# Reordering the seven products of a two-by-two block multiplication, and starting their weight sums with the stage

## The chip, the core and the metric

One core of a Trainium2 chip runs the whole program. The metric is the device time of one execution in microseconds (us). The kernel before takes 3117.28 us, the median of three runs (3116.49 to 3119.43).

The engines that matter here are TensorE (PE in the rows: matmuls, transposes), VectorE (DVE), ScalarE (ACT), GpSimd (POOL) and SyncE (SP). Each takes its own instructions strictly in the order in which they stand in its program; an instruction that waits holds up everything behind it on that engine. SP does nothing here but start the plain transfers, POOL starts the transfers that add to what is already in the buffer.

## What is computed

A network of six layers on 256 tokens of width 1024, in fp32: four layers of FFN, attention, FFN (eight FFNs) and two further layers of a mixer and one FFN each. All ten FFNs have the same core:

```
def swiglu(x, w_in, w_out):
    gate, up = jnp.split(x @ w_in, 2, axis=-1)
    return (jax.nn.silu(gate) * up) @ w_out
```

`w_in` is 1024 x 5632 (gate and up beside each other, 2816 columns each), `w_out` 2816 x 1024. Around it stand norms, residuals and, once in between, the attention or the mixer. 34.6 MB of weights are read for each FFN and used for 256 tokens only, so that the weights are streamed through the core once.

## The kernel before

**Precision.** A matmul runs on fp32r operands, which keep fewer bits than fp32. Each operand is therefore split into a high and a low part: ACT casts the high part (L171), DVE subtracts to get the low part (L172), and `mm3` issues three matmuls, high x high (L220), low weight x high x (L222) and high weight x low x (L224).

**Tiles.** The tokens form two tiles of 128 (t = 0, 1). The 2816 columns of an FFN are cut into 11 chunks of 256 (gate and up of a chunk make 512 columns, one PSUM bank). `f1(c, t)` multiplies tile t with chunk c, 24 matmuls, and starts a small task `hidden` (tanh on ACT at L414, two DVE steps at L416 and L417 that write `hd`, a transpose of `hd` on PE at L252, the split into `hT`). `f2` multiplies `hT` with 256 rows of `w_out` and adds into the accumulators aA (t = 0) and aB (t = 1), 12 matmuls.

**Seven products for eight.** Two pairs of neighbouring chunks of each FFN (4 and 5, 8 and 9) are not computed by `f1`. `seven(c)` takes tokens in two halves, the depth 1024 in two halves, and makes gate and up of both chunks and both tiles from seven products in place of eight. It needs seven sums of halves of x, made once per stage by `halves_of_x` (the tiles Sh and Sl, in the order 0, 1, 2, 3, 5, 4, 6), and for some products sums of quarters of the weights (a quarter is 512 deep x 512 wide, 1 MB). A sum of quarters is not computed by an engine: `load` (L449, SP) brings one quarter into a buffer `rs`, and `plus` (L454, POOL) starts two transfers of 512 KB that add another quarter to it in place. `split` casts the result, `block` multiplies it with one of the seven sums, 12 matmuls. The two `rs` buffers y and z go through chains: y is first B01+B00 (product 3), then another quarter is added (product 4), then another (product 2); z is B11 (product 6), then plus B01 (product 5). A `plus` has to wait until the split before it has read the buffer, and the next split has to wait until the `plus` has landed. Products 0 and 1 use single quarters, loaded into the common `raw` buffers.

**What sets the order.** In `ffn` a string gives the order around each seven: "fo7of7o7fo7of7o7o7o", where f is an `f1`, o an `f2` and 7 the next product. The products come in the order 0, 1, 3, 4, 6, 5, 2, and the first part of `seven` (load of y, first `plus`, load of z) runs just ahead of the string; for the first seven of a stage that is after the four opening `f1` (chunks 0 and 1, both tiles) and after `halves_of_x`. The tile framework then places each engine's instructions by its own cost model, so that the order on an engine is not the order of the text.

**Buffers.** Four `raw` buffers (RAW_BUFS) of 1 MB take all plain weights, seven hi/lo pairs (W_BUFS) the casts. `halves_of_x` uses an `rs` buffer for its scratch f (L582). In the stages behind the first, `ada_step` reads 1 MB of `w_ada` into a `raw` buffer twice per seven and multiplies it on DVE (L1182, L1184).

The sixteen stages (ten FFNs, four attentions, two mixers) are numbered from 0. The one shown below is stage 3, the second layer's first FFN, directly behind the first layer's last: its `f1` begin at 563 us of the profile and it ends near 750 us.

Of the kernel before, what the change touches and what calls it, by code (L numbers as in the profile page):

```python
# [18 lines left out]
P = 128  # L19
D = 1024  # L20
S = 256
# [13 lines left out]
UW = 1024  # L35

RAW_BUFS = 4
# [65 lines left out]
class _Net:  # L103
# [296 lines left out]
    def ffn(self, w_in, w_out, factors, finish, middle, scaled):  # L400
# [33 lines left out]
        def seven(c):  # L434
# [1 line left out]

            S = sums["S"]

            def quarter(k, n):
                return self.cols(w_in, c * FC + n * DFF, 512, 4 * k, 4)

# [8 lines left out]
            def plus(r, k, n):  # L452
                for q in range(2):
                    nc.gpsimd.dma_start(r[:, 2 * q : 2 * q + 2], quarter(k, n)[:, 2 * q : 2 * q + 2], accum_op=ALU.add)  # L454
# [8 lines left out]
                return ws  # L463

            def block(i, ws):
                ps = self.ps("mm")
                x = ([S[0][:, i, k] for k in range(4)], [S[1][:, i, k] for k in range(4)])
                for k in range(4):
                    self.mm3([(ps, slice(0, 512))], x, k, ws[k], k == 0, k == 3)
                return ps  # L470

            def add(dst, u, v):
                nc.vector.tensor_tensor(dst, u, v, op=ALU.add)

            def tile(ps=None):
                r = self.t(self.mp, [P, 512], "sc", bufs=3)
                if ps is not None:
                    nc.scalar.copy(r, ps)
                return r
# [13 lines left out]
            plus(y, 0, 0)  # L493
            z = load(1, 1)
            yield
            s = tile(block(0, split(load(0, 0, True))))
            yield
            g0 = self.t(self.fp, [P, 512], "res", bufs=2)
            add(g0, block(1, split(load(1, 0, True))), s)
            gate(g0)  # L500
            ws = split(y)
            plus(y, 1, 1)
            yield
            u1 = tile(block(3, ws))
            ws = split(y)
            plus(y, 1, 0)
            yield
            add(s, block(4, ws), s)
            u0 = tile()
            add(u0, s, u1)  # L510
            ws = split(z)
            plus(z, 0, 1)
            yield
            add(u0, block(6, ws), u0)
            self.start(out(0, g0, u0))
            yield
            add(s, block(5, split(z)), s)
# [11 lines left out]
            f2(c, t=t)  # L529

        first = ((0, 0), (0, 1), (1, 0), (1, 1)) if self.stage == 0 else ((0, 0), (1, 0), (0, 1), (1, 1))
        for c, t in first:
            f1(c, t)
        queue.extend((c, t) for c in range(2) for t in range(NT))
        self.start(self.halves_of_x(sums, scaled))
        for plain, c in PLAN:


            gen = seven(c)
            next(gen)  # L540
            others = [(r, t) for r in plain for t in range(NT)]
            for n, what in enumerate("fo7of7o7fo7of7o7o7o"):
                if what == "f":
                    f1(*others[0])
                    queue.append(others.pop(0))
                elif what == "o":
                    pop()
                else:
                    self.force(lambda: "S" in sums)
                    next(gen, 0)  # L550
                if n in (6, 15) and self.stage > 0:
                    self.ada_step()
            queue.extend((c + i, t) for i in range(2) for t in range(NT))
            if middle:
                middle()
                middle = None
# [8 lines left out]
    def halves_of_x(self, res, scaled):  # L565


        nc = self.nc
        if not scaled:
            fs = [self.prepared(t) for t in range(NT)]  # L570
            rb = self.t(self.mp, [P, NT, P], "rb")
            ps = self.ps("tp")
            for t in range(NT):
                nc.tensor.matmul(ps[:, t * P : t * P + P], fs[t][:, 0:1].to_broadcast([P, P]), self.ident,
                                 start=True, stop=True)
            nc.scalar.copy(rb, ps[:, :S].rearrange("p (a b) -> p a b", a=2))
        S_ = [self.t(self.mp, [P, 7, 4, P], f"S{n}", F32R) for n in "hl"]

        def put(i, v):
            self.hilo(v, S_[0][:, i], S_[1][:, i])  # L580

        f = self.t(self.mp, [P, 4, 512], "rs", bufs=2)  # L582
        x = {}
        for t in (0, 1):
            for k in (0, 1):
                xh, xl = (v[:, 4 * k : 4 * k + 4].bitcast(F32) for v in self.xT[t])
                v = x[t, k] = f[:, 2 * t + k].rearrange("p (a b) -> p a b", a=4)
                nc.vector.tensor_tensor(v, xh, xl, op=ALU.add)
                if not scaled:
                    nc.vector.tensor_tensor(v, v, rb[:, t, None, :].to_broadcast([P, 4, P]), op=ALU.mult)  # L590
        tt, stt = nc.vector.tensor_tensor, nc.vector.scalar_tensor_tensor
        put(0, x[0, 0])
        put(1, x[0, 1])
        put(2, x[1, 1])
        tt(x[1, 1], x[1, 1], x[1, 0], op=ALU.subtract)
        put(3, x[1, 1])
        tt(x[1, 0], x[0, 0], x[1, 0], op=ALU.subtract)
        put(5, x[1, 0])
        stt(x[0, 0], x[1, 1], -1.0, x[0, 0], op0=ALU.mult, op1=ALU.subtract)
        put(4, x[0, 0])  # L600
        stt(x[0, 1], x[0, 0], -1.0, x[0, 1], op0=ALU.mult, op1=ALU.subtract)
        put(6, x[0, 1])
        res["S"] = S_
        return
        yield
# [1005 lines left out]
```

## Time and profile before

| | us |
|---|---|
| median of three runs | 3117.28 (3116.49 to 3119.43) |
| the profiled execution, whole | 3114.58 |
| its span, first to last instruction | 3112.8 |
| PE busy | 2890.8 (93%) |
| DVE busy | 2177.3 (70%) |
| ACT busy | 1669.8 (54%) |
| POOL busy | 432.7 (14%) |
| mean granted TensorE clock | 0.967 |
| moved by DMA, mean over the span | 203 GB/s |

"Busy" is time in which an engine has an instruction under way. PE is idle for 222 us of the span. The granted clock is the share of full speed at which the chip lets TensorE run: it is 1.0 most of the time and 0.5 for some microseconds after some of the waits, so a mean of 0.967 is time lost too, beside the idle time and not in it.

### The profile page before, as it was taken

The page shows a single profiled execution, that of the slowest core. Times are in us where ns is not written, and L with a number is a line of the kernel's source. Part 1 is how long each engine was busy: PE and PEld are TensorE (multiplying, and loading weights), DVE is VectorE, ACT ScalarE, POOL GpSimd, SP SyncE. Part 2 cuts the span into 40 slices and gives each one's busy share as a digit, 9 for nine tenths or more (in the row PEclk, how much of TensorE's full clock was granted, in tenths as well). Part 3 has the DMA queues.
Part 4 walks back from the last instruction along what each step waited for, and adds up shares of the span by engine and source line. Part 5 has one row for each costly group of instructions (what it writes and reads, how often), then busy time and mean ns, then how long its engine had stood idle before and what let it go on. Part 6 is the DMA issues. An engine that isn't in the chain of part 4 may idle for free.

```text
span 3112.8 us, 36892 instructions
## 1 busy us (share of the span) xinstructions
PE 2890.8 (93%) x13165; PEld 2308.1 (74%) x13165; DVE 2177.3 (70%) x3275; ACT 1669.8 (54%) x2853; POOL 432.7 (14%) x601
## 2 busy tenths in 40 slices
PE   7999989999998998999989889998999998999888
PEld 6787767777786786778767768776778777788677
DVE  7675867767567686666867867586776687865766
ACT  5456645545665454456645545664555454644544
POOL 1112110111111011121100111211111011100110
PEclk9999999999999999999999999999999999999999
DMA  9754587786458778651687786458765589665784
GB/s 281 216 177 148 173 253 203 237 243 181 152 167 239 210 231 250 190 187 54 192 236 201 231 237 195 136 185 249 225 212 177 170 252 267 212 221 169 209 244 129
DMA packets 358043, 633.27 MB, mean 203 GB/s; under 512 B 15170, under 2 KB 190132, under 8 KB 357860
## 3 DMA queue, kind: packets, MB, share of 16 engines
q1 hardware_dynamic: 312724, 541.99, 50.9%
q0 software_dynamic: 44768, 88.30, 16.0%
q8 instruction: 104, 1.70, 0.2%
q14 instruction: 79, 0.65, 0.1%
q10 hardware_dynamic: 368, 0.62, 0.1%
HBM read 629.82 MB, written 1.05 MB: 203 GB/s over the span
## 4 chain that ended last, share of the span: by engine, by line
PE 52%; DMA 18%; issue 17%; DVE 7%; ACT 4%; POOL 2%; ACTq 0%; SPq 0%; POOLq 0%; DVEq 0%
DMA rs<-in_ffn_w_in_dram 13%; PE mm L222 10%; PE mm L224 10%; PE mm L220 10%; DVE lo L172 4%; DMA rs<-in_w_ffn_in_dram 4%; PE tp L252 3%; PE aA L222 2%; PE aA L220 2%; PE aA L224 2%; ACT hi L171 2%; PE aB L224 2%; PE aB L220 2%; PE aB L222 2%; DMA raw<-in_w_ada_dram 1%
## 5 line engine op out<-in xcount | busy, mean ns | idle before, releaser
L172 DVE TENSOR_TENSOR lo<-raw,hi 128x1024 fp32r<-128x1024 f32 x834 | 1004.2, 1219 | 240.4 <-ACT hi L171 232.5
L171 ACT CAST hi<-raw 128x1024 fp32r<-128x1024 f32 x834 | 867.2, 1050 | 393.9 <-PE mm L224 201.7
L220 PE MATMUL mm<-hi,xh 128*128 128x512 f32 (+2 forms) x1856 | 762.0, 412 | 112.6 <-ACT hi L171 112.0
L222 PE MATMUL mm<-lo,xh 128*128 128x512 f32 (+2 forms) x1856 | 747.5, 403 | 12.4 <-DVE lo L172 12.0
L224 PE MATMUL mm<-hi,xl 128*128 128x512 f32 (+2 forms) x1856 | 740.6, 399 | 2.0 <-DVE xl L172 1.0
L220 PEld LDWEIGHTS mm<-hi,xh 128*128 128x128 f32 x1856 | 359.1, 194 | 199.5 <-ACT hi L171 127.9
L222 PEld LDWEIGHTS mm<-lo,xh 128*128 128x128 f32 x1856 | 358.4, 193 | 102.8 <-DVE lo L172 36.8
L224 PEld LDWEIGHTS mm<-hi,xl 128*128 128x128 f32 x1856 | 358.3, 193 | 79.5 <-DVE xl L355 5.0
L171 ACT CAST hi<-rs 128x1024 fp32r<-128x1024 f32 x200 | 207.0, 1049 | 324.4 <-DMA rs<-in_ffn_w_in_dram 246.3
L172 DVE TENSOR_TENSOR lo<-rs,hi 128x1024 fp32r<-128x1024 f32 x200 | 241.6, 1221 | 187.9 <-ACT hi L171 186.1
L454 POOL DMA_DIRECT2D rs<-in_ffn_w_in_dram x128 | 155.9, 1285 | 1049.1 <-DVE lo L172 845.4
L220 PE MATMUL mm<-hi,Sh 128*128 128x512 f32 x560 | 229.0, 409 | 0.0
L222 PE MATMUL mm<-lo,Sh 128*128 128x512 f32 x560 | 223.1, 398 | 0.0
L224 PE MATMUL mm<-hi,Sl 128*128 128x512 f32 x560 | 222.2, 397 | 0.0
L220 PE MATMUL aB<-hi,hT 128*128 128x512 f32 x568 | 202.3, 417 | 0.0
L220 PE MATMUL aA<-hi,hT 128*128 128x512 f32 x584 | 198.2, 402 | 1.3 <-DVE s L658 0.9
L222 PE MATMUL aB<-lo,hT 128*128 128x512 f32 x568 | 198.9, 407 | 0.0
L224 PE MATMUL aB<-hi,hT 128*128 128x512 f32 x568 | 195.5, 405 | 0.9 <-DVE hT L268 0.8
L222 PE MATMUL aA<-lo,hT 128*128 128x512 f32 x584 | 193.0, 394 | 0.6 <-DVE lo L172 0.5
L264 ACT CAST hT<-tp 128x256 fp32r<-128x256 f32 x268 | 95.1, 371 | 183.3 <-PE tp L252 183.2
L224 PE MATMUL aA<-hi,hT 128*128 128x512 f32 x584 | 192.0, 392 | 0.0
L265 DVE TENSOR_TENSOR hT<-tp,hT 128x256 fp32r<-128x256 f32 x268 | 107.9, 417 | 53.2 <-ACT hT L264 52.7
(280 smaller groups left out, 3666.8 us busy)
## 6 DMA issues: line engine op xcount, KB each, us to landing
raw<-in_ffn_w_in_dram SPq DMA_DIRECT2D x224, 512.0 KB, 5.3
raw<-in_ffn_w_out_dram SPq DMA_DIRECT2D x88, 1024.0 KB, 7.1
rs<-in_ffn_w_in_dram POOLq DMA_DIRECT2D x128, 512.0 KB, 7.9
raw<-in_w_ada_dram SPq DMA_DIRECT2D x48, 1024.0 KB, 9.2
raw<-in_w_in_dram SPq DMA_DIRECT2D x44, 1024.0 KB, 5.2
rs<-in_ffn_w_in_dram SPq DMA_DIRECT2D x32, 1024.0 KB, 6.7
raw<-in_ffn_w_in_dram SPq DMA_DIRECT2D x32, 1024.0 KB, 6.8
raw<-in_w_ffn_in_dram SPq DMA_DIRECT2D x56, 512.0 KB, 4.9
```

The source lines that it names most:

```text
L171: self.nc.scalar.copy(hi, raw)
L172: self.nc.vector.tensor_tensor(lo, raw, hi.bitcast(F32), op=ALU.subtract)
L220: mm(ps, xh[k], wh[:, c], start=first, stop=False)
L222: mm(ps, xh[k], wl[:, c], start=False, stop=False)
L224: mm(ps, xl[k], wh[:, c], start=False, stop=last)
L252: self.nc.tensor.transpose(dst, src, self.ident[:k, :k])
L264: nc.scalar.copy(hi, v)
L265: nc.vector.tensor_tensor(lo, v, hi.bitcast(F32), op=ALU.subtract)
L454: nc.gpsimd.dma_start(r[:, 2 * q : 2 * q + 2], quarter(k, n)[:, 2 * q : 2 * q + 2], accum_op=ALU.add)
```

## The change

The seven products come in the order 6, 3, 0, 1, 4, 5, 2. Product 6 uses z as it was loaded and product 3 the first sum in y, and behind each of these two splits the next `plus` is started at once. Between product 3 and product 4 (the next link of y) now stand products 0 and 1, between 6 and 5 (the next link of z) stand five, and between 4 and 2 stands 5. The string becomes "fo77fo7o7fo7o7foo7no"; the new letter n runs the first part of the next seven (load of y, `plus`, load of z). The first part of a stage's first seven runs ahead of the four opening `f1`. `halves_of_x` takes a `raw` buffer for f. The first `ada_step` of a string comes one letter later. The products' sums are kept in the same three `sc` tiles; product 6 now stands first, so ACT copies it out of PSUM (one more copy for each seven), and some DVE additions read `sc` where they read PSUM.

```diff
             y = load(0, 1)
             plus(y, 0, 0)
             z = load(1, 1)
+            yield
+            u0 = tile(block(6, split(z)))
+            plus(z, 0, 1)
+            yield
+            u1 = tile(block(3, split(y)))
+            plus(y, 1, 1)
+            add(u0, u0, u1)
             yield
             s = tile(block(0, split(load(0, 0, True))))
             yield
             g0 = self.t(self.fp, [P, 512], "res", bufs=2)
             add(g0, block(1, split(load(1, 0, True))), s)
             gate(g0)
-            ws = split(y)
-            plus(y, 1, 1)
             yield
-            u1 = tile(block(3, ws))
-            ws = split(y)
+            add(s, block(4, split(y)), s)
             plus(y, 1, 0)
-            yield
-            add(s, block(4, ws), s)
-            u0 = tile()
-            add(u0, s, u1)
-            ws = split(z)
-            plus(z, 0, 1)
-            yield
-            add(u0, block(6, ws), u0)
+            add(u0, u0, s)
             self.start(out(0, g0, u0))
             yield
             add(s, block(5, split(z)), s)
...
         first = ((0, 0), (0, 1), (1, 0), (1, 1)) if self.stage == 0 else ((0, 0), (1, 0), (0, 1), (1, 1))
+        gens = [seven(c) for _, c in PLAN]
+        next(gens[0])
         for c, t in first:
             f1(c, t)
...
-            gen = seven(c)
-            next(gen)
+            gen, after = gens.pop(0), gens[:1]
             others = [(r, t) for r in plain for t in range(NT)]
-            for n, what in enumerate("fo7of7o7fo7of7o7o7o"):
+            for n, what in enumerate("fo77fo7o7fo7o7foo7no"):
...
+                elif what == "n":
+                    for g in after:
+                        next(g)
                 else:
                     self.force(lambda: "S" in sums)
                     next(gen, 0)
-                if n in (6, 15) and self.stage > 0:
+                if n in (7, 15) and self.stage > 0:
                     self.ada_step()
...
-        f = self.t(self.mp, [P, 4, 512], "rs", bufs=2)
+        f = self.t(self.wp, [P, 2 * UW], "raw", bufs=RAW_BUFS).rearrange("p (a b) -> p a b", a=4)
```

The number of matmuls and of transfers is the same. What the framework makes of the new text is seen in three places.

On ACT, in the first seven of stage 3, before: both casts of the buffer y for product 3 (hi<-rs), then W_out's, then both casts of y for product 4, and only then the casts of chunk 3 (raw_1283 in the last row) that `f1(3, 0)` needs.

```order
L171 CAST hi_1263_5273<-rs_1215_5080 128x1024
L171 CAST hi_1265_5277<-rs_1215_5080 128x1024
L171 CAST hi_1268_5285<-raw_1267_5283 128x1024
L171 CAST hi_1270_5289<-raw_1267_5283 128x1024
L414 ACTIVATE th_1253_5240<-mm_1252_5215,fs1_1162_4819 128x256
L171 CAST hi_1279_5334<-rs_1215_5080 128x1024
L171 CAST hi_1281_5338<-rs_1215_5080 128x1024
L483 ACTIVATE res_1262_5270<-res_1255_5245 128x512
L171 CAST hi_1284_5347<-raw_1283_5344 128x1024
```

The same engine now, begun six rows behind the second cast of y for product 3 (raw_1278 is the single quarter of product 1, raw_1285 and raw_1290 are chunk 3, and the last row is the first cast of y for product 4):

```order
L171 CAST hi_1279_5339<-raw_1278_5337 128x1024
L171 CAST hi_1281_5343<-raw_1278_5337 128x1024
L414 ACTIVATE th_1256_5256<-mm_1255_5231,fs1_1162_4823 128x256
L171 CAST hi_1286_5367<-raw_1285_5364 128x1024
L171 CAST hi_1288_5371<-raw_1285_5364 128x1024
L264 CAST hT_1267_5298<-tp_1266_5295 128x256
L476 COPY sc_1269_5305<-mm_1265_5285 128x512
L171 CAST hi_1291_5378<-raw_1290_5375 128x1024
L171 CAST hi_1293_5382<-raw_1290_5375 128x1024
L171 CAST hi_1298_5428<-rs_1167_4839 128x1024
```

The cast that waits for y's second sum stood ahead of chunk 3's casts and four rows behind the cast of y's first sum; it now stands behind all four of chunk 3's and fifteen rows behind.

On DVE, where the sums of x are finished in stage 3 (Sl is written for the seven sums in turn, the last of them sum 6), before:

```order
L601 SCALAR_TENSOR_TENSOR rs_1214_5053<-rs_1214_5053 128x512
L417 SCALAR_TENSOR_TENSOR hd_1232_5142<-hd_1232_5142,fs0_1148_4729,mm_1227_5108 128x256
L172 TENSOR_TENSOR Sl_1213_5052<-rs_1214_5053,Sh_1212_5051 128x512
L172 TENSOR_TENSOR lo_1244_5176<-raw_1240_5169,hi_1243_5175 128x1024
L172 TENSOR_TENSOR Sl_1213_5052<-rs_1214_5053,Sh_1212_5051 128x512
L265 TENSOR_TENSOR hT_1248_5193<-tp_1246_5189,hT_1247_5192 128x256
L172 TENSOR_TENSOR lo_1258_5249<-raw_1256_5246,hi_1257_5248 128x1024
```

and now, where lo_1241 and lo_1243 belong to z for product 6, lo_1250 and lo_1252 to y for product 3, and `ada` is the work on `w_ada`:

```order
L600 SCALAR_TENSOR_TENSOR raw_1216_5063<-raw_1216_5063 128x512
L172 TENSOR_TENSOR Sl_1215_5062<-raw_1216_5063,Sh_1214_5061 128x512
L417 SCALAR_TENSOR_TENSOR hd_1232_5146<-hd_1232_5146,fs0_1148_4733,mm_1227_5112 128x256
L172 TENSOR_TENSOR lo_1237_5156<-raw_1233_5149,hi_1236_5155 128x1024
L172 TENSOR_TENSOR lo_1241_5174<-rs_1168_4843,hi_1240_5173 128x1024
L172 TENSOR_TENSOR lo_1243_5178<-rs_1168_4843,hi_1242_5177 128x1024
L265 TENSOR_TENSOR hT_1247_5195<-tp_1245_5191,hT_1246_5194 128x256
L172 TENSOR_TENSOR lo_1250_5206<-rs_1167_4839,hi_1249_5205 128x1024
L1181 TENSOR_SCALAR ada_1275_5329<-raw_1276_5330,col_235_236_1007 128x512 x2
L172 TENSOR_TENSOR lo_1252_5210<-rs_1167_4839,hi_1251_5209 128x1024
```

Before, the first product (0) used sum 0, written long before this place; now the first product (6) uses sum 6, the last one written, and its low weights lo_1241 come after that. The work on `w_ada` stands between the two halves of y's split, and its buffer is free only when the last Sl has been written (f lies in it).

On SP, at the start of the program, before (raw_24 and raw_29 are the two halves of chunk 0, each loaded by two transfers, raw_49 the first half of chunk 1):

```order
L276 DMA cst_1_76<-in_const_dram 128x264
L280 DMA h0_2_78<-in_x_dram 128x1024
L182 DMA raw_24_144<-in_ffn_w_in_dram 128x4x256 x2
L182 DMA raw_29_155<-in_ffn_w_in_dram 128x4x256 x2
L182 DMA raw_49_270<-in_ffn_w_in_dram 128x4x256 x2
```

and now (the two `rs` are y and z of the first seven):

```order
L276 DMA cst_1_76<-in_const_dram 128x264
L280 DMA h0_2_78<-in_x_dram 128x1024
L182 DMA raw_26_150<-in_ffn_w_in_dram 128x4x256
L447 DMA rs_18_107<-in_ffn_w_in_dram 128x4x512
L447 DMA rs_19_111<-in_ffn_w_in_dram 128x4x512
L182 DMA raw_26_150<-in_ffn_w_in_dram 128x4x256
L182 DMA raw_31_161<-in_ffn_w_in_dram 128x4x256 x2
```

Two loads of 1 MB now stand between the two transfers of the very first weights. In the later stages y and z stand behind chunk 1's second half (after an attention or a mixer: chunk 1's first half in three of them) or between the two halves of chunk 0, and the two `plus` of y stand on POOL in the chain of small steps that ends the stage before (L316, L317, L307).

## Rows read from the trace of the kernel before

**Rows 1.** The page, part 1: busy us, share of the span, instructions.

```profile
PE 2890.8 (93%) x13165; PEld 2308.1 (74%) x13165; DVE 2177.3 (70%) x3275; ACT 1669.8 (54%) x2853; POOL 432.7 (14%) x601
```

**Rows 2.** Waits of PE, whole span: us in total, times, longest us.

```profile
PE mm L220 <- ACT hi L171: 113.1, 22, 7.6
PE tp L252 <- DVE hd L417: 40.1, 18, 4.5
...
PE mm L222 <- DVE lo L172: 12.0, 21, 1.2
```

**Rows 3.** Timeline of PE, stage 3: start, us, line, operation, [idle before <-releaser].

```profile
623.44 0.79 PE L220 MATMUL mm<-hi,xh 128*128 128x512 f32 x1 [7.01 <-ACT hi L171]
...
703.41 0.69 PE L220 MATMUL mm<-hi,xh 128*128 128x512 f32 x1 [4.57 <-ACT hi L171]
```

**Rows 4.** Timeline of ACT, the same place, columns as in rows 3.

```profile
620.88 1.04 ACT L171 CAST hi<-rs 128x1024 fp32r<-128x1024 f32 x1 [4.29 <-DMA rs<-in_ffn_w_in_dram]
...
622.36 1.03 ACT L171 CAST hi<-raw 128x1024 fp32r<-128x1024 f32 x1
```

**Rows 5.** Timeline of POOL, the same place: the two transfers of one plus.

```profile
606.24 2.44 POOL L454 DMA_DIRECT2D rs<-in_ffn_w_in_dram  x2 [24.69 <-DVE lo L172]
```

**Rows 6.** DMA issues of 606 to 609 us: count, KB each, us to landing.

```profile
rs<-in_ffn_w_in_dram POOLq DMA_DIRECT2D x2, 512.0 KB, 11.3
```

**Rows 7.** Busy us (instructions) by engine, granted clock, DMA share, GB/s, three stretches.

```profile
595.00:615.00 20.00, 20.00 (x90) 16.18 (x89) 17.83 (x26) 10.50 (x14) 2.44 (x2) 1.00 0.66 200
...
623.40:628.40 5.00, 4.79 (x10) 3.31 (x11) 5.00 (x6) 3.68 (x5) 2.41 (x2) 0.50 0.30 38
...
703.40:710.30 6.90, 6.09 (x13) 4.02 (x14) 6.90 (x10) 3.12 (x5) 1.20 (x1) 0.51 0.67 117
```

**Rows 8.** Page, costliest groups: xcount, busy us, mean ns, idle before and its releasers.

```profile
L172 DVE TENSOR_TENSOR lo<-rs,hi 128x1024 fp32r<-128x1024 f32 x200 | 241.6, 1221 | 187.9 <-ACT hi L171 186.1
```

**Rows 9.** Timeline of PE, start of the program: the first matmuls on weights.

```profile
11.86 0.80 PE L220 MATMUL mm<-hi,xh 128*128 128x512 f32 x1 [4.19 <-ACT hi L171]
13.12 0.80 PE L222 MATMUL mm<-lo,xh 128*128 128x512 f32 x1 [0.46 <-DVE lo L172]
```

**Rows 10.** Waits of DVE, whole span, columns as in rows 2.

```profile
DVE ada L1184 <- DMA raw<-in_w_ada_dram: 39.0, 7, 6.3
```

**Rows 11.** Timeline of PE, stage 3: the first matmul of the first product.

```profile
596.38 0.40 PE L220 MATMUL mm<-hi,Sh 128*128 128x512 f32 x1
```

**Rows 12.** Timeline of DVE, stage 3: the end of the sums of x.

```profile
590.65 2.49 DVE L590 TENSOR_TENSOR rs<-rs,rb 128x512 f32<-128x512 f32 x4
...
600.24 1.22 DVE L172 TENSOR_TENSOR lo<-raw,hi 128x1024 fp32r<-128x1024 f32 x1
601.38 0.69 DVE L172 TENSOR_TENSOR Sl<-rs,Sh 128x512 fp32r<-128x512 f32 x1
```

**Rows 13.** Page, part 6: count, KB each, us to landing, of two loads.

```profile
raw<-in_w_ada_dram SPq DMA_DIRECT2D x48, 1024.0 KB, 9.2
...
rs<-in_ffn_w_in_dram SPq DMA_DIRECT2D x32, 1024.0 KB, 6.7
```

**Rows 14.** Columns as in rows 7: the start of the program.

```profile
8.00:20.00 12.00, 7.68 (x26) 5.89 (x27) 8.34 (x16) 9.62 (x22) 4.05 (x9) 1.00 1.08 359
```

**Rows 15.** Timeline of PE, end of stage 1: the last transposes of the attention.

```profile
341.50 0.38 PE L252 MATMUL tp<-cst,on 128*128 128x128 f32 x2
```

**Rows 16.** Timeline of POOL, ends of stages 1 and 7: the norm's small steps.

```profile
348.39 1.09 POOL L316 TENSOR_SCALAR s<-s 128x1 f32<-128x1 f32 x1
350.40 0.82 POOL L317 TENSOR_SCALAR s<-s,s 128x1 f32<-128x1 f32 x1 [0.92 <-ACT junk L315]
...
1495.48 0.27 POOL L317 TENSOR_SCALAR s<-s,s 128x1 f32<-128x1 f32 x1 [0.61 <-ACT junk L315]
```

**Rows 17.** Columns as in rows 7: stage 3 whole, and its densest 20 us.

```profile
563.20:750.50 187.30, 169.79 (x725) 133.88 (x725) 142.26 (x193) 97.06 (x138) 22.93 (x23) 0.95 0.80 234
...
600.00:620.00 20.00, 16.43 (x74) 13.08 (x72) 12.86 (x17) 8.34 (x11) 2.44 (x2) 1.00 0.93 275
```

More of the change, by code (lines that the diff above doesn't have):

```diff
@@ L434, in seven @@
         def seven(c):
-            S = sums["S"]
             def quarter(k, n):
@@ L465, in block @@
             def block(i, ws):
-                ps = self.ps("mm")
+                ps, S = self.ps("mm"), sums["S"]
                 x = ([S[0][:, i, k] for k in range(4)], [S[1][:, i, k] for k in range(4)])
```

## The prediction, made before the changed kernel ran

> **What bounds the kernel now.** The page's busy times come first: PE 2890.8 us of 3112.8, no other engine above 70% [rows 1]. Time can only come from PE's 222 idle us and from its clock, so the next view is what PE waited for. Two lines stand out: 113.1 us in 22 waits of a matmul for a cast on ACT, with 12.0 us in 21 waits for the low weights that follow, and 40.1 us in 18 waits of a transpose for `hd` from DVE [rows 2]. One wait of each of the first two is the start of the program; the other 20 and 20 lie one in each seven.
>
> The timelines show what such a wait is. At 623.44 PE has been idle for 7.01 us [rows 3]. The matmul belongs to `f1(3, 0)`, whose weights landed long before; their cast on ACT runs at 622.36, behind two casts of the buffer y, of which the second alone waited 4.29 us for its transfer [rows 4]. Those are the two transfers of a `plus`, started at 606.24 [rows 5], which took 11.3 us to land by the median of the two [rows 6]. They could not start earlier, since the split of the link before reads the buffer until then, and between the two links PE has one product and one `f1` to do, some 8 us. The second seven waits 4.57 us at 703.41 in the same way [rows 3].
>
> A wait also costs afterwards. Before it PE starts 90 matmuls in 20.00 us at full clock; in the 5.0 us behind the first wait the clock is 0.50 and in the 6.9 us behind the second 0.51, which are the lower of the two levels (1.2 and 2.4 GHz), with 10 and 13 matmuls [rows 7]. At half speed half the time is lost: 2.5 and 3.5 us, 3.0 on the mean.
>
> **The change, part by part.** All sums are made against the profiled execution, 3114.58 us, which is 2.7 below the median of 3117.28.
>
> *The links.* A link needs its split (1.05 us a cast [rows 4] and 1.22 a subtraction [rows 8], twice), the start of two transfers (2.44 [rows 5]) and their landing (11.3 [rows 6]): about 15 us from the first cast's release to the second landing. Between products 3 and 4 PE now has an `f1` (24 matmuls, 5.3 us at the 0.222 us of [rows 7]), 0, an `f2`, 1, an `f1` and an `f2` (12 each, 2.7 us): 21 to 22 us. Between 4 and 2 it has an `f2`, 5, an `f1` and two `f2`, 16 us; between 6 and 5 over 25. All three cover it, the link from 4 to 2 just. ACT's casts of chunk 3 now stand ahead of the waiting cast, as its order shows. So I take both groups of 20 waits away: 113.1 + 12.0, less the 4.65 us at the start (4.19 and 0.46 [rows 9]), is **-120.5**. With them goes the half clock, 20 x 3.0 = **-60** (-50 to -70 by the two stretches). What is late next, if cover fails, is product 2: at worst 2 us a seven, 40 in all.
>
> *The transposes for `hd`.* Many of these come from DVE standing at L1184 for a load of `w_ada` (39.0 us in 7 waits [rows 10]), with `hd` queued behind it. With the links gone, DVE and ACT run less bunched, and in the second seven the load starts earlier against its use; in the first it is started later (below). The bounds are 0 and -40; I take half, **-20**, being able to follow only some of them.
>
> *The first product.* This is a new wait. Product 6 needs the last sum of x. Before, the first product started at 596.38 without a wait [rows 11], while the last Sl was written at 601.38 to 602.07 [rows 12]. That end moves forward: one subtraction of 1.22 us (600.24) goes from ahead of it, and the quarters no longer cast before it free DVE so that L590 can start about 1 us before its 590.65 [rows 12]; it ends at about 600, its high part at 599. Then DVE has W_out's subtraction and z's, 2.4 us, until 602.4. PE comes to product 6 after 16 matmuls of the two `f2`, at 597.3. It waits 1.6 us for the high part, does six more of `f2`, and waits again 1.4 us for z's low weights: 3.0. Behind it, y's second subtraction stands behind two instructions on `w_ada`, whose load is held by f in the `raw` buffer until the last Sl, so that it starts at 600 only. It takes 9.2 us on the median [rows 13], and the second subtraction would then come 3.6 us after PE wants it; nothing else is queued ahead of it there, and at 6 us or less the wait is 0.3. I take 0.8, near the lower end. For a clock that falls now and then I add 0.8 (a third of the shorter loss of [rows 7]). Ten stages x 4.6 = **+46**, with bounds of 0 (product 6 meets other work first) and 75.
>
> *The start of the program.* y and z, 2 MB, now stand between the two halves of the first weights. Transfers run without a gap there, 359 GB/s at a share of 1.08 [rows 14]: 2 MB are 5.9 us, and the first matmul moves from 11.86 [rows 9] to about 18. **+6**, with bounds 4 and 9; nothing hides it.
>
> *The ends of the attentions.* On POOL y's `plus` waits for y inside the norm's chain, and L317 behind it holds the residual and the next stage's first transposes. What decides is when y is loaded. Its buffer is free after the last transposes of the attention, 341.50 [rows 15], and SP starts it then; with the median of 6.7 us for such a load [rows 13] y lands at 348.6. So the `plus` waits for little, but its two starts (2.44 us) behind L316, which ends at 349.5, put L317 at 352.0 for 350.40 [rows 16]: 1.6 us, in two stages. In the stage behind the third attention y lands at about 1495, the two starts lie ahead of L316 and L317, and L317 moves from 1495.48 [rows 16] to 1497.7: 2.2. In the second attention's and the mixers' ends I find 0 to 0.5. **+6**, with bounds 0 and 25. Behind FFNs y lands 10 us before it matters. The 20 extra copies on ACT (54% busy) and f's place cost nothing by themselves.
>
> Sum: 3114.6 - 120.5 - 60 - 20 + 46 + 6 + 6 = 2972.1, and with the 2.7 us to the median 2974.8, say **2975**.
>
> **The rivals.**
>
> *All of it (A).* No wait for `hd` is left and product 6's wait is hidden: 2975 - 20 - 46 = 2909. For it: both waits rest on where single instructions stand. Against it: the DVE row that product 6 needs is the last of a full queue.
>
> *The transfers become the bound (B).* Stage 3 takes 187.3 us at a DMA share of 0.80 [rows 17], 150 us of transfers; my sum makes it some 171 us, a share of 0.88. The densest 20 us reach 0.93 and 275 GB/s [rows 17]. If a whole stage can hold no more than 0.85, it takes 176.3 us and gains 11: 3114.6 - 110 + 12 + 2.7 = 3019. Against it: y, z and one `plus` of a stage leave the dense part for the light end of the stage before.
>
> By the Trainium skill, page "DMA: Bandwidth & Descriptors", section "Specifications", a core has about 358 GB/s from HBM and 435 GB/s at its ports, so that a stage at 234 GB/s would be far from full and B would have no chance. The trace does not agree: 275 GB/s were already a share of 0.93, so B keeps its chance.
>
> *Slower (C).* SP's queue is in order and the `raw` buffers are four, one of which f now holds until 600 us; `w_ada`, product 1's quarter and chunk 3 stand behind it on SP. If this lateness reaches PE in each seven as a wait of 10 us with the 3.0 of the clock, 20 x 13 = 260 go against the net gain of 142: 3235. The point is 7.1 us a seven. Against it: by the order chunk 3 would land at 616 and 621 us and be used from 623 on, and the second seven has no f.
>
> *No link gets longer on the chip (D)*, the waits only moving to other casts: about 3117.
>
> **How the numbers follow.** Forecast 0.62; A 0.11; B 0.17; C 0.06; D 0.04. The forecast's own range is 2935 to 3030 (from the clock, `hd` and product 6). 8 in 10: down to 2925, which leaves out most of A, and up to 3045, which takes in most of B. A measurement of this kernel can tell 0.2%, 6 us, from no change. Faster by more than that: 0.62 + 0.11 + 0.17 = 0.90; within it: D with 0.03; slower: C and the rest of D, 0.07.
>
> **What would show it.** Right: the line of matmuls waiting for ACT's casts falls from 113.1 to under 40 us, and the casts hi<-rs no longer wait for a transfer with PE idle; the mean clock rises from 0.967 to about 0.985; a first product that waits 1 to 2 us twice in each stage; the first matmul at 18 us; L317 1.6 us later behind two attentions. Wrong: a DMA share near 0.9 with casts hi<-raw waiting for transfers (B), L182's loads starting later against the products (C), or a wait of more than 3 us for product 2 or for z in the second seven, whose load starts only behind product 2's split.

## The result, and the profile after

The changed kernel takes 2964.47 us (median of four runs, 2963.95 to 2965.05), the kernel before on the same chip 3116.89 us: a ratio of 0.9513, with an interval of 0.9497 to 0.953. The forecast was 2975 in a range of 2925 to 3045. It held, but one of its reasons did not.

The page of the changed kernel, part 1 (busy us, share, instructions), and its span and mean clock:

```profile
PE 2842.5 (96%) x13165; PEld 2280.9 (77%) x13165; DVE 2183.1 (74%) x3275; ACT 1686.3 (57%) x2873; POOL 427.2 (14%) x601
...
core 0: 2963.3 us, clock 0.988
```

Against [rows 1] PE has as many instructions and 48.3 us less busy time: the same matmuls at a higher clock (0.988, before 0.967). The span is 149.5 us shorter, so 101.2 of them are idle time, 222.0 before and 120.8 now. The waits of PE in the changed kernel (us in total, times, longest us) say which:

```profile
PE tp L252 <- DVE hd L417: 19.1, 15, 3.7
...
PE mm L222 <- DVE lo L172: 12.0, 15, 4.0
PE mm L220 <- ACT Sh L171: 10.7, 6, 1.8
PE aA L222 <- DVE lo L172: 7.7, 6, 1.3
PE mm L220 <- ACT hi L171: 7.2, 5, 5.0
PE mm L220 <- ACT sc L476: 5.6, 5, 2.1
```

The line that held 113.1 us in [rows 2] holds 7.2, of which 5.0 are the start of the program. `hd` fell from 40.1 to 19.1. New are the two lines of the first product, Sh and aA<-lo, six waits each. The low weights (L222) are still 12.0, but at other places: one wait of 4.0 and fourteen of 0.3 to 0.9.

The same from ACT's side, its waits for the `rs` buffers, before and now:

```profile
ACT hi L171 <- DMA rs<-in_ffn_w_in_dram: 246.3, 61, 8.8
```

```profile
ACT hi L171 <- DMA rs<-in_ffn_w_in_dram: 6.8, 4, 2.3
```

Before, two of the three links of a seven were waited for on ACT, y's to product 4 and z's to product 5; the 113.1 us are behind the first of them.

Where the link stood. POOL of the changed kernel starts z's and y's second additions in stage 3 here (start, us, [idle before <-releaser]):

```profile
579.12 2.51 POOL L452 DMA_DIRECT2D rs<-in_ffn_w_in_dram  x2 [30.99 <-issue]
584.45 1.20 POOL L452 DMA_DIRECT2D rs<-in_ffn_w_in_dram  x1 [2.83 <-DVE lo L172]
586.38 1.20 POOL L452 DMA_DIRECT2D rs<-in_ffn_w_in_dram  x1 [0.73 <-DVE lo L172]
```

The rows at 584.45 and 586.38 start the next link of y. The DMA issues of 584 to 587.6 us (count, KB each, us to landing) have them as

```profile
rs<-in_ffn_w_in_dram POOLq DMA_DIRECT2D x2, 512.0 KB, 9.6
```

so they land at about 594 and 596. On PE product 3 ends at 587.7: the two transfers start 3.2 and 1.3 us ahead of its end. ACT casts them for product 4 here:

```profile
603.86 1.04 ACT L171 CAST hi<-rs 128x1024 fp32r<-128x1024 f32 x1
609.75 1.05 ACT L171 CAST hi<-rs 128x1024 fp32r<-128x1024 f32 x1 [0.89 <-PE aB L224]
```

Neither cast waits for a transfer, where the one of [rows 4] waited 4.29 us. The second waits 0.89 us for PE to give back a buffer. The link has some 10 us to spare.

What the change cost. PE and ACT at stage 3's first product:

```profile
575.15 0.50 PE L220 MATMUL mm<-hi,Sh 128*128 128x512 f32 x1 [1.78 <-ACT Sh L171]
577.49 0.73 PE L222 MATMUL aA<-lo,hT 128*128 128x512 f32 x2 [1.30 <-DVE lo L172]
```

```profile
573.97 1.13 ACT L171 CAST Sh<-raw 128x512 fp32r<-128x512 f32 x2
```

PE starts product 6 (at 575.15) in the moment in which ACT has cast the last sum of x (573.97 + 1.13 = 575.10). The pair of 1.78 and 1.30 us (1.18 once) returns in six of the ten FFNs and is absent from four.

The start of the program, and POOL and PE behind the first attention:

```profile
18.61 1.22 PE L220 MATMUL mm<-hi,xh 128*128 128x512 f32 x2 [5.01 <-ACT hi L171]
```

```profile
341.61 1.20 POOL L316 TENSOR_SCALAR s<-s 128x1 f32<-128x1 f32 x1
342.87 2.52 POOL L452 DMA_DIRECT2D rs<-in_ffn_w_in_dram  x2
344.48 1.22 POOL L317 TENSOR_SCALAR s<-s,s 128x1 f32<-128x1 f32 x1
```

```profile
348.71 0.66 PE L252 MATMUL tp<-cst,h 128*128 128x128 f32 x4 [0.97 <-DVE h L383]
```

The first matmul on weights comes 6.75 us later than in [rows 9]. The two starts of `plus` stand between L316 and L317 as the prediction had it, and PE waits 0.97 us for the residual that hangs on them.

Last, stage 3 as a whole and its dense part (columns as in [rows 7]):

```profile
539.10:710.40 171.30, 164.80 (x726) 131.03 (x725) 142.95 (x193) 99.09 (x140) 20.38 (x21) 0.99 0.82 240
...
600.00:620.00 20.00, 17.94 (x77) 13.87 (x76) 17.52 (x22) 11.04 (x14) 2.39 (x2) 1.00 1.05 323
```

The stage, 187.3 us in [rows 17], takes 171.3. Its 20 us from 600 reach 323 GB/s at a share of 1.05, with the clock at 1.00, so the share of 0.93 in [rows 17] was no ceiling.

### The profile page after: what moved, and what is told of

It is laid out like the page before. It is cut to its first block, busy times and chain, and to the rows that moved or that the text cites. A ratio compares the mean times of both kernels' runs of the same rounds, so it can differ in the third digit from the quotient of the medians.

```text
span 2963.3 us, 36815 instructions
## 1 busy us (share of the span) xinstructions
PE 2842.5 (96%) x13165; PEld 2280.9 (77%) x13165; DVE 2183.1 (74%) x3275; ACT 1686.3 (57%) x2873; POOL 427.2 (14%) x601
## 3 DMA queue, kind: packets, MB, share of 16 engines
HBM read 629.82 MB, written 1.05 MB: 213 GB/s over the span
## 5 line engine op out<-in xcount | busy, mean ns | idle before, releaser
L220 PE MATMUL mm<-hi,xh 128*128 128x512 f32 (+2 forms) x1856 | 746.1, 404 | 10.3 <-ACT hi L171 5.6
L222 PE MATMUL mm<-lo,xh 128*128 128x512 f32 (+2 forms) x1856 | 730.7, 394 | 3.4 <-DVE lo L172 3.4
L224 PE MATMUL mm<-hi,xl 128*128 128x512 f32 (+2 forms) x1856 | 729.2, 393 | 1.9 <-DVE xl L172 1.0
L220 PEld LDWEIGHTS mm<-hi,xh 128*128 128x128 f32 x1856 | 350.8, 189 | 88.2 <-ACT hi L171 10.1
L224 PEld LDWEIGHTS mm<-hi,xl 128*128 128x128 f32 x1856 | 350.6, 189 | 78.3 <-DVE xl L355 4.8
L222 PEld LDWEIGHTS mm<-lo,xh 128*128 128x128 f32 x1856 | 351.4, 189 | 76.4 <-DVE lo L172 12.3
L220 PE MATMUL mm<-hi,Sh 128*128 128x512 f32 x560 | 231.5, 413 | 13.3 <-ACT Sh L171 10.7
L222 PE MATMUL mm<-lo,Sh 128*128 128x512 f32 x560 | 227.4, 406 | 8.7 <-DVE lo L172 8.7
L222 PE MATMUL aA<-lo,hT 128*128 128x512 f32 x584 | 195.7, 398 | 7.7 <-DVE lo L172 7.7
L222 PE MATMUL aB<-lo,hT 128*128 128x512 f32 x568 | 191.1, 396 | 0.0
L224 PE MATMUL aB<-hi,hT 128*128 128x512 f32 x568 | 190.1, 393 | 0.8 <-DVE hT L268 0.8
L220 PE MATMUL aB<-hi,hT 128*128 128x512 f32 x568 | 190.5, 398 | 0.0
```

The lines of the kernel that those rows point to most:

```text
L220: mm(ps, xh[k], wh[:, c], start=first, stop=False)
L222: mm(ps, xh[k], wl[:, c], start=False, stop=False)
L224: mm(ps, xl[k], wh[:, c], start=False, stop=last)
```

## The experiments

Twelve kernels, each compared with the kernel before in runs on the same chip. Ratios are therefore to be compared, and not the last us.

**e1, e2: the early start and the order, apart.** e1 is the changed kernel with the first part of a stage's first seven put back behind the four `f1`:

```diff
-        next(gens[0])
         for c, t in first:
             f1(c, t)
         queue.extend((c, t) for c in range(2) for t in range(NT))
         self.start(self.halves_of_x(sums, scaled))
+        next(gens[0])
```

> The changed kernel with one part undone: the first part of a stage's first seven (load of y, its plus, load of z) runs where it ran before, behind the four opening f1 and the sums of x. Theory (the new order of the products is what counts): the links stay covered, the 5 us at the start of the program and the 0.8 to 1.0 us behind three attentions come back, and y's first sum is still landed when product 3 wants it; 2950 to 2970, against 2964.5 of the changed kernel. Rival (starting with the stage counts for itself, by moving 3 MB of transfers of each stage out of its dense part): product 6 or 3 or chunk 2 waits for its load in each stage, at least 3 us with the clock in ten stages, so 2995 or more.

Measured: 2959.97 us, 0.9503 (0.9478 to 0.9528). The early start is worth nothing that can be told from noise; without it the first matmul on weights is back at 11.99 us.

e2 is the kernel before with that early start and with f in `raw`, in the old order.

> The kernel before with that part alone: the first part of a stage's first seven runs with the stage, and the scratch of the sums of x lies in a raw buffer; products and string are those of before. Theory: the links are as close as before, so the 20 waits for casts stay (90 us or more in that line of PE's waits) and the time is 3095 to 3130. Rival (starting early is worth 30 us or more): below 3087.

Measured: 3107.43 us, 0.9983 (0.997 to 0.9996). Waits of PE:

```profile
PE mm L220 <- ACT hi L171: 108.4, 22, 7.8
PE tp L252 <- DVE hd L417: 40.5, 20, 4.3
```

Nearly the lines of [rows 2], and 0.2% of time. Nearly all of the gain is in the order of the products and of their splits.

**e3, e4: what the links cost in all.** Both leave out the later additions of each seven (y's second and third quarter, z's second; 120 of 160 adding transfers), so that products 4, 2 and 5 work on incomplete sums:

```diff
-            plus(z, 0, 1)
-            plus(y, 1, 1)
-            plus(y, 1, 0)
```

e3 does so in the kernel before, e4 in the changed one.

> The kernel before without the second and third plus of y and the second quarter of z (products 4, 2 and 5 use what lies in the buffer): 6 MB of slow transfers less for each stage and no link to wait for. Theory (the long waits are the landing of these transfers): both groups of 20 waits and their half clock go, 3117 - 180 = 2937, within 20 either way. Rival (the waits are ACT's and DVE's queues, whatever lands): above 3050.

> The changed kernel without the same three plus: the same 6 MB less for each stage. Theory (the links are covered and the transfers are no bound): within 12 us of 2964.5. Rival (the transfers have become the bound of the stage, 0.88 to 0.9 of a stage): they free 25 us or more of each stage's transfers, so 2925 or less.

Measured: e3 2889.62 us, 0.9275; e4 2931.69 us, 0.9414. Waits of PE in e4:

```profile
PE mm L220 <- ACT Sh L171: 10.7, 6, 1.8
PE tp L252 <- DVE hd L417: 9.5, 14, 1.4
```

Two things follow. The links cost the kernel before some 7% (1 - 0.9275), about 220 us. That is more than the 180 of -120.5 and -60, so they also cost time elsewhere. And they still cost the changed kernel 1%, some 31 us (0.9513 - 0.9414), which lies between e4's two theories, though no cast of its links waits long: its waits for `hd` halve without them, from 19.1 to 9.5, and so do ACT's waits for plain weights, as these lines of the changed kernel and of e4 show:

```profile
ACT hi L171 <- DMA raw<-in_ffn_w_in_dram: 61.4, 26, 6.2
```

```profile
ACT hi L171 <- DMA raw<-in_ffn_w_in_dram: 27.5, 20, 3.3
```

So the additions delay plain loads in this order. They do not do so in every order: the same line holds 1.6 us in the kernel before and 7.6 in e11 below, which have all the additions. The difference between e4 and e3, 1.4% or 42 us, is the price of the new order where no link matters: first product, start, attention ends and whatever else it moves.

**e5, e6: another first product.** Order 0, 3, 6, 1, 4, 5, 2, so that the first product needs no late sum; e5 with the late start of e1, e6 with the early one.

```diff
-            u0 = tile(block(6, split(z)))
-            plus(z, 0, 1)
+            s = tile(block(0, split(load(0, 0, True))))
             yield
             u1 = tile(block(3, split(y)))
             plus(y, 1, 1)
-            add(u0, u0, u1)
             yield
-            s = tile(block(0, split(load(0, 0, True))))
+            u0 = tile(block(6, split(z)))
+            plus(z, 0, 1)
+            add(u0, u0, u1)
```

> The changed kernel with another order of the first products, 0, 3, 6, 1, 4, 5, 2, and the late start of e1: product 0 needs the first sum of x and a single quarter, as before the change. Theory (the new waits of the changed kernel are product 6 waiting for the last sum): PE's waits for Sh (10.7 us), for low weights inside the f2 beside it (7.7) and for the sc copy (5.6) go, with 10 to 15 us of half clock: 2960 of e1 less 30, so 2920 to 2945. Rival (they move on to product 3 or 6, whose weights now come later): 2955 or more.

> The same order of products, with the early start of the changed kernel. Theory: the early start only costs its 5 us at the start of the program and some 3 us behind three attentions, so 3 to 10 us above e5. Rival (the early start lightens the dense part and is worth something once the first product no longer waits): below e5 by 5 us or more.

Measured: 2956.2 us, 0.9504, and 2954.29 us, 0.9493 (0.947 to 0.9515). The waits for Sh are gone, and this took their place in e6:

```profile
PE mm L222 <- DVE lo L172: 18.5, 25, 2.3
PE aA L222 <- DVE lo L172: 15.7, 6, 2.6
```

aA<-lo rose from 7.7 to 15.7, the other low weights from 12.0 to 18.5: 14.5 more for the 10.7 that went. DVE is full at this place (busy for 13.1 of the 14 us from 566 in the changed kernel), and product 0 in the first place does not avoid it.

**e8: the sixth sum written sooner** (the sums of x in the order 0, 1, 2, 6, 3, 5, 4).

> The changed kernel with the seven sums of x written in the order 0, 1, 2, 6, 3, 5, 4, so that the sum of the first product comes three splits (0.68 us of DVE each) sooner; products unchanged. Theory: the wait for Sh (1.78 us in six stages) falls under 0.5, the wait for z's low weights behind it (1.30) stays or grows a little, since DVE still does all of Sl first; 2948 to 2962. Rival (the wait is not the sum but z's cast): no change in the wait for Sh, 2960 to 2970.

Measured: 2966.03 us, 0.9531, and the wait is the same 1.78 us in six places. It is inconclusive on its question: sum 6 is the last link of a chain of subtractions, and the framework placed it as late as before. In stage 3 DVE makes its value until 570.4, and ACT casts it from 570.6 on, directly behind.

**e7: a link with little work between.** The prediction held that a link of 15 us needs as much work of PE between its two products, and that the 16 us from product 4 to 2 just cover it. e7 leaves 8.

```diff
-            for n, what in enumerate("fo77fo7o7fo7o7foo7no"):
+            for n, what in enumerate("fo77fo7o7fo7o7o7fono"):
```

> The changed kernel with one f1 and one f2 moved from ahead of product 2 to behind it, so that only an f2, product 5 and an f2, 8 us, stand between products 4 and 2; the sum for product 2 needs 13 to 15 us from its split to its landing. Theory (what counts is the PE work between two links): a wait of 5 to 7 us and 2.5 to 3 of half clock come back in each of 20 sevens, 3110 to 3165. Rival (distance is not the lever, the early plus or ACT's order is): within 20 of 2964.5.

Measured: 2964.7 us, 0.9526 (0.9501 to 0.955), the time of the changed kernel. PE does have less to do there: in stage 3 product 4 ends at 609.8 and product 2 begins at 618.5, 8.7 us, where the changed kernel has 17.1 (614.9 to 631.9). Yet no long wait came back. Waits of ACT for the transfers of a link in e7, and its cast of the second half for product 2:

```profile
ACT hi L171 <- DMA rs<-in_ffn_w_in_dram: 4.2, 3, 1.5
```

```profile
618.24 1.05 ACT L171 CAST hi<-rs 128x1024 fp32r<-128x1024 f32 x1 [1.26 <-DMA rs<-in_ffn_w_in_dram]
```

The work of PE between two products is thus not the whole cover of a link: a `plus` waits for the split and not for the product, and the split runs ahead of PE. The two transfers of this link start at 603.19 and 608.43, both before product 4 ends, and the second lands 9.7 us later, at 618.1. That is just in time, with nothing to spare.

In the kernel before, too, the `plus` starts at 606.24 [rows 5], while PE ends product 3 at 616.4 only (623.44 less the 7.01 idle us of [rows 3]). What then held PE at 623.44? The place of the next cast: before, the split for product 4 is written a product early, so that its cast stands on ACT ahead of chunk 3's.

**e9, e10: the place of the cast alone.** e9 is the kernel before with one thing moved, the split for product 4 to where product 4 is issued. The order of products stays, and 8 us between 3 and 4.

```diff
             u1 = tile(block(3, ws))
-            ws = split(y)
-            plus(y, 1, 0)
             yield
-            add(s, block(4, ws), s)
+            add(s, block(4, split(y)), s)
+            plus(y, 1, 0)
```

> The kernel before with one edit: the split of the second sum of y (for product 4) is written where product 4 is issued, and no longer one step earlier, ahead of an f1 and an f2. The products keep their old order, and between products 3 and 4 PE still has only one f1 and one f2, some 8 us. ACT's order then has the casts of chunk 3 ahead of the two casts of y. Theory 'place in ACT's queue': the harm of before was that the waiting cast stood ahead of the casts of the next f1, whose weights had landed; the split of product 3 is done 10 us before product 3 ends on PE (606.2 against 616.3), so that with the f1 and f2 behind it there are 18 us for a link of 15. Matmuls waiting for hi fall from 113.1 to under 20 us, most of the half clock goes, 2935 to 2985. Theory of my prediction, 'distance': a link of 15 us needs as much work of PE between the two products; with 8 us the missing 7 us a seven stay and only move to product 4: 3060 to 3115.

e10 moves, beside that, one f2 from behind product 4 to ahead of it.

> As e9, and one f2 moved from behind product 4 to ahead of it, so that PE has 2.7 us more between products 3 and 4 (10.7 for 8). By the queue theory the cover was enough already: within 8 us of e9. By the distance theory 2.7 us of each of 20 waits go: some 40 to 54 us under e9.

Measured: e9 3053.47 us, 0.9799 (0.9768 to 0.9831); e10 3040.3 us, 0.976 (0.9737 to 0.9783). Neither theory's number: the f2 is worth 0.4%, 13 us, where the queue theory had under 8 and the distance theory 40 to 54, and the two intervals overlap. Waits of PE in e9, and the longest line of e10:

```profile
PE tp L252 <- DVE hd L417: 85.9, 29, 4.9
PE mm L222 <- DVE lo L172: 30.6, 19, 4.4
...
PE mm L220 <- ACT hi L171: 6.3, 4, 3.3
```

```profile
PE mm L222 <- DVE lo L172: 78.5, 51, 6.2
```

The line of ACT's casts fell from 113.1 to 6.3 as the queue theory has it, but `hd` rose from 40.1 to 85.9. In e10 `hd` has only 5.3, and the low weights have 78.5: the waiting moved to another line, and little of it went. One wait for `hd` in e9, on POOL, ACT, DVE and PE in turn:

```profile
613.62 2.55 POOL L454 DMA_DIRECT2D rs<-in_ffn_w_in_dram  x2 [0.16 <-issue]
```

```profile
621.74 1.05 ACT L171 CAST hi<-rs 128x1024 fp32r<-128x1024 f32 x1 [5.32 <-DMA rs<-in_ffn_w_in_dram]
626.40 1.05 ACT L171 CAST hi<-rs 128x1024 fp32r<-128x1024 f32 x1 [3.62 <-PE aB L224]
627.36 0.47 ACT L414 ACTIVATE th<-mm,fs 128x256 f32<-128x256 f32 x1
```

```profile
629.08 0.48 DVE L417 SCALAR_TENSOR_TENSOR hd<-hd,fs,mm 128x256 f32<-128x256 f32 x1
```

```profile
629.61 0.44 PE L252 MATMUL tp<-cst,hd 128*128 128x128 f32 x2 [1.85 <-DVE hd L417]
```

The `plus` at 613.62 is z's, the link from product 6 to 5. With y's link out of the way it ends last: products 6 and 5 have one f2 between them, the two casts on ACT come 8.1 and 12.8 us after 613.62, and the tanh of an `f1` (L414) stands behind them. The second cast is put down to PE, but the trace has the second transfer's landing at 626.33, 0.07 us ahead of it: of several things waited for, the row names one.

The kernel before has the same wait already, shorter and in fewer places. In its stage 2, on ACT and PE (the tanh is at 436.87):

```profile
435.91 1.05 ACT L171 CAST hi<-rs 128x1024 fp32r<-128x1024 f32 x1 [3.84 <-DMA rs<-in_ffn_w_in_dram]
```

```profile
439.12 0.44 PE L252 MATMUL tp<-cst,hd 128*128 128x128 f32 x2 [2.65 <-DVE hd L417]
```

Counted by this mark, a transpose 3.2 us behind the start of z's second cast, the kernel before has seven such waits, 10.0 of the 40.1 us, and e9 fifteen, 53.7 of the 85.9. The difference is nearly the whole rise of the line.

**e11, e12: z's link freed, then y's squeezed.** e11 is e9 with product 6, and the `plus` behind it, put ahead of product 3: order 0, 1, 6, 3, 4, 5, 2. The 8 us between 3 and 4 stay.

```diff
+            u0 = tile(block(6, split(z)))
+            plus(z, 0, 1)
+            yield
             u1 = tile(block(3, ws))
+            add(u0, u0, u1)
             yield
             add(s, block(4, split(y)), s)
             plus(y, 1, 0)
-            u0 = tile()
-            add(u0, s, u1)
-            ws = split(z)
-            plus(z, 0, 1)
-            yield
-            add(u0, block(6, ws), u0)
+            add(u0, u0, s)
...
-            for n, what in enumerate("fo7of7o7fo7of7o7o7o"):
+            for n, what in enumerate("fo7of7o77fo7of7oo7o"):
```

> e9 with product 6 moved from behind product 4 to ahead of product 3 (order 0, 1, 6, 3, 4, 5, 2; one f2 goes from ahead of product 5 to behind it), so that the link of z from 6 to 5 has product 3, two f1, two f2 and product 4 of PE's work, some 21 us, where e9 has one f2. The distance from 3 to 4 stays one f1 and one f2. If the rest of e9's loss is the link of z (its cast waited 5.32 us for the two transfers, and the subtraction behind it stood ahead of hd on DVE), the waits for hd fall from 85.9 to under 30 us and the time to 2940 to 2975 (ratio 0.943 to 0.955). If the rest is the short distance from 3 to 4, it stays within 15 us of e9: 3040 to 3070.

e12 takes away the f1 and f2 between 3 and 4 ("fo7of7o777foof7oo7o").

> e11 with the f1 and the f2 between products 3 and 4 moved to behind product 4, so that these two stand next to each other on PE and only the lead of product 3's split (4 to 8 us) and product 3 itself lie against a link of 15 us. If distance decides at all once the cast stands where it is used, each of 20 sevens waits 4 to 8 us more, with 3 us of half clock behind it: 140 to 220 us over e11. If only the place of the cast in the queues matters, it is within 15 us of e11.

Measured: e11 2950.56 us, 0.948 (0.9466 to 0.9495); e12 2976.16 us, 0.9559 (0.9543 to 0.9575). e11 has the whole gain, and a little more than the change, without moving products 3 and 4 apart, without the early start and with product 0 first. One thing more than z's link changed in it: the split for product 3 and the `plus` behind it keep their place in the text, so that they now stand ahead of product 6. In stage 3 that `plus` starts at 569.68 and product 4 at 592.0, 22 us later. The 8 us of matmuls are therefore not all of this link's cover. ACT waits 2.8 us in all for these transfers in e11, and of the `hd` waits counted above none is left, as in the changed kernel. Waits of PE in e11:

```profile
PE tp L252 <- DVE hd L417: 29.2, 12, 4.4
PE mm L222 <- DVE lo L172: 28.8, 21, 4.0
...
PE mm L220 <- ACT hi L171: 5.4, 2, 4.3
```

The lines of Sh and aA<-lo are absent. e12, with no work at all between the two products, loses 26 us against e11 (0.8%), not 140 to 220. Its rows in stage 3 show the mechanism of the whole case once more (ACT, DVE, PE):

```profile
591.71 1.04 ACT L171 CAST hi<-rs 128x1024 fp32r<-128x1024 f32 x1 [4.86 <-DMA rs<-in_ffn_w_in_dram]
592.66 0.62 ACT L483 ACTIVATE res<-res 128x512 f32<-128x512 f32 x1
```

```profile
593.31 0.69 DVE L484 SCALAR_TENSOR_TENSOR res<-res,res 128x512 f32<-128x512 f32 x1 [6.11 <-ACT res L483]
...
594.58 1.22 DVE L172 TENSOR_TENSOR lo<-rs,hi 128x1024 fp32r<-128x1024 f32 x1
```

```profile
595.86 0.79 PE L222 MATMUL mm<-lo,Sh 128*128 128x512 f32 x1 [5.83 <-DVE lo L172]
```

ACT waits 4.86 us for y's link, a tanh for product 1's result (L483) stands behind that cast, L484 on DVE waits for it 6.11 us, and behind L484 stands a subtraction that PE wants for product 6, which has nothing to do with this link. So too little cover makes the cast wait, and what stands behind the cast decides where PE pays for it and how much.

## Why the prediction was right, and where it was not

- **What bounds the kernel, and in what way: right.** PE's waits for casts behind waiting casts were the cost, and their clock with them. The prediction's own view of the trace ([rows 3] to [rows 6]) names the queue of ACT.
- **Links, -120.5: the direction right, 14.6 too much.** 113.1 became 7.2, that is -105.9. (Of the 22 waits, one of 1.13 us lay in no seven; it is still there.) The 20 waits for low weights that I took away went with them, but the line stayed at 12.0, since others came: eight of 0.5 to 0.9 us for the second half of product 4's weights, six of 0.3 to 0.6 in an `f1`, and one of 3.98 at 2465.86. There z's second subtraction, for product 6 of a second seven, stands on DVE behind work on `w_ada` that waits 3.61 us for its load.
- **The reason for it: wrong.** "Between products 3 and 4 PE now has ... 21 to 22 us" and "the link from 4 to 2 just" reckon a link against PE's work between its products. By e7 8 us are as good as 16, by e11 8 us with the cast at its place do as well as 21, and by e12 none at all costs 26 us. The link begins with the split: its first transfer starts some 10 us before the product ends on PE in the kernel before, where the split is written a product early, and 3.2 us before in the changed kernel. What a waiting cast costs is decided by what is queued behind it. The prediction had both halves of this in its text (the split releases the `plus`; chunk 3's casts now stand ahead), and took the wrong one for its sum. It also missed z's link, which holds 10.0 us of the `hd` line before and ends last as soon as only y's is freed (53.7 us in e9).
- **Clock, -60: right within its size.** PE's busy time fell by 48.3; with the 8 us added for the first product my net was -52.
- **`hd`, -20: right**, 40.1 to 19.1, though half was a choice between two bounds, and the 10.0 us behind z's link were not seen: the prediction put the line down to `w_ada`. e4 shows that half of the rest hangs on the links' transfers.
- **First product, +46: the waits right, their number wrong.** 1.6 and 1.4 us were forecast, 1.78 and 1.30 measured, but in six FFNs of ten: 18.4 us. Waits for the copy of a product (L476), four of five in an `f1`, add 5.6, which I had not listed. The second subtraction of y behind the work on `w_ada`, for which I took 0.8 each, has no line of its own; the one long wait of this kind is z's of 3.98 above. e4 less e3 puts first product, start and attention ends, with whatever else the order moves, at 42 us, where I had 58.
- **Start, +6: right** (6.75). **Ends of the attentions, +6: half of it.** Three waits of 0.97, 0.98 and 0.80 us, 2.75, where I had 1.6, 1.6 and 2.2. Behind the first attention L317 starts 1.67 us after L316 has ended, for 0.92 in [rows 16]: 0.75 later, where I had 1.6.
- **Rival B** had the transfers as the bound at a share of 0.85. The stage of 171.3 us, which I had put at some 171, has 0.82, and 20 us of it 1.05 at 323 GB/s. So 0.85 was no bound, and B's 0.17 was too much; [rows 14], which I had used for the start, already held 359 GB/s at a share of 1.08. The Trainium skill's rule that was cited there ("DMA: Bandwidth & Descriptors", section "Specifications", about 358 GB/s from HBM for a core) would have said so. The trace agrees with it: 323 GB/s over 20 us.

The sum of these errors is small: 14.6 too much on the links, some 16 too much for the costs. These two nearly cancel, so that the nearness is partly luck.

What stays open: the changed order with its splits written a product early was not tried, so that the shares of order and place within the change itself are known only from the side of the kernel before (e9: 2.0%, with z's link moved 5.2%). How much of e11's step over e9 is z's link, and how much the earlier split for product 3, was not taken apart. Why four FFNs of ten have no wait at the first product was not followed up.

## What to carry to other kernels

When PE waits for a cast whose input landed long ago, look for the instruction ahead of it in the same engine's queue that waits for a transfer, and first try to write that one where its result is used; here moving one split and one product (e11) was worth as much as the reordering. Reckon a transfer's cover from the instruction that releases it, not from the matmuls that come after. And take away the waits of one chain only after looking which chain ends next: e9 has less than half of e11's gain, since z's link, which held 10.0 us of PE's waits before, held 53.7 once y's was gone.

## What the runs showed of the hardware

Additions in place have a price that hidden landing does not remove: without the 120 later ones (e4 against the changed kernel) the same kernel is some 31 us faster. They take more of the DMA engines' time than plain loads do. The queues of the kernel before (packets, MB, share of 16 engines' time over the span; q1 has SP's plain transfers, q0 those that POOL starts, nearly all of them additions):

```profile
q1 hardware_dynamic: 312724, 541.99, 50.9%
q0 software_dynamic: 44768, 88.30, 16.0%
```

Over 3112.8 us that is some 342 GB/s of busy time for the one and 177 for the other, an estimate from these two rows. What the additions do to plain loads depends on how densely they lie: such a load of 512 KB has a median of 6.4 us from issue to landing in the changed kernel and 5.1 in e4, but 5.3 in the kernel before and 5.0 in e3.
